# A hybrid diffusion backbone on one core: the layer-1 modulation product is summed per partition by VectorE and closed by TensorE, with changes to splits, a context write and the row ends

## The chip, the cores and the metric

The kernel runs on one core of a Trainium2 chip. The metric is the device time of one execution in microseconds, taken as the median of several runs. The engines are named as in the profile: PE is TensorE (PEld its weight loads), DVE is VectorE, ACT is ScalarE, POOL is GpSimd, and SP is the engine that issues nearly all DMA transfers. Each engine works through its own queue in order.

## What is computed

Two layers (`DEPTH` 2) of a backbone with 1024 features, 512 latent tokens and 256 context tokens. The modulation vector `c` (and `c_ctx` for the context) goes through one matrix per layer and yields six rows of 1024 features, which shift, scale and gate the two halves of a layer:

```python
mod   = silu(c)     @ w_mod[i] + b_mod[i]     # (1, 6 * 1024)
mod_c = silu(c_ctx) @ w_mod[i] + b_mod[i]
x = LN(alpha * x + gate1 * Mixer(modulate(x, shift1, scale1)))
x = LN(alpha * x + gate2 * (square(relu(h @ w1)) @ w2))   # h = modulate(x, shift2, scale2)
```

The mixer is one input projection, a conformer convolution, a bidirectional chunked state-space scan (SSD) and one output projection of 1536 to 1024 features. The MLP has 4096 hidden features. The output is the latent stream after two layers, in float32.

## The kernel before

**Matmuls and splits.** Every large matmul has float32 accuracy by three passes over operands that are split in a high and a low part. A weight unit of 512 KB is loaded to `raw`, cast by ScalarE to the high half of a buffer (L300), and the low half is the difference (L301), on VectorE, or for every third unit of an output projection on GpSimd (`sub_engine`, L272, unless `ostate["late"]` is set). The buffers are `spl`, of which there are three, and `splx`, which takes every fourth unit in output projections and MLPs. `weight()` keeps two units ahead.

**Output projection** (`outproj`, L849). Its left operand is split per feature block into `cr` (two buffers): the high half by ScalarE (L866), the low half alternately by GpSimd and VectorE (L868). TensorE's matmuls are L888. A finished half is multiplied by the gate, added to the residual and given to the row statistics on VectorE (L895 to L897). In layer 0 a first call does context and half of the latents (its branch ends with L910, which stops the modulation steps), a second call the rest; in the last layer there is no context.

**MLP** (`mlp`, L940). Eight chunks of 512 hidden features: the first matrix (L962), relu and square (L950 to L954), then the second matrix (L969), twelve tiles of twelve matmuls per chunk, each added to `acc` by VectorE (L1025). In the last chunks the residual is added (`residual`, L1202 to L1207) and `finish` (L1212) makes the row ends.

**Modulation.** The product for a layer is three parts of 2048 columns. A step (`mod_step`, L155) loads a row block of 128 x 2048 (1 MB, each partition one run of 8 KB) into an `spl` buffer under the name `mraw`, and makes four matmuls of 512 columns each with the two rows of `c` as the stationary operand, `tile_position` placing them in four column groups of the array (L160). After eight steps a part is complete in the PSUM bank `pm`; bias, transposes and the copies to `modT` and `grow` follow. Layer 1 needs 24 steps. They are queued in `fill` at the output projection of layer 0 and taken by `tick()` (L192), which is called after each block of work: at every tick in the first output projection (`FILLO` 1), at every fourth tick in the MLP (`FILLM` 4). The matmuls of a step follow three ticks behind the load (`MLAG`). What is left at chunk 6 is drained by `mod_rest`.

**Row ends.** In the last layer a finished row tile of 128 tokens is normalised: `FSPL` says how many of its 1024 columns VectorE does (0, 0, 512, 1024 for the four tiles); the rest is done by ScalarE (L1237) and GpSimd (L1238, L1239), then stored. GpSimd also makes each tile's `rsy`, the inverse standard deviation (L320). In layer 0, `finish` writes each pair of tiles as `xn` to memory with two GpSimd operations per tile (L1253, L1254), for latents and context.

The order on each engine comes from a scheduler that takes the operations by priority; `tc.cur_priority` shifts a stretch of code, and a higher number is later.

Of the kernel before, what the change touches and what calls it, by code (L numbers as in the profile page):

```python
# [7 lines left out]
F32 = mybir.dt.float32  # L8
# [7 lines left out]
DM = 1024  # L16
# [27 lines left out]
FILLM = 4  # L44
# [34 lines left out]
def block(ctx, tc, a):  # L79
# [40 lines left out]
    wdt = const.tile([128, DEPTH, 8, 32], F32, name="wdt")  # L120
    nhalf = const.tile([128, 8], F32, name="nhalf")
# [30 lines left out]
    def mod_step(l, part, kt, raw=None):  # L152
# [9 lines left out]
        if kt < 7:  # L162
            return
# [28 lines left out]
    def tick(mod_ok=True):  # L192
# [12 lines left out]
        if mod_wait and mod_wait[0][0] <= clock["t"]:  # L205
            mod_step(*mod_wait.popleft()[1])
        if mod_ok and fill and clock["t"] % clock["fill"] == 0:
            f = fill.popleft()
            lag = MLAG[state["x"] is not None]
            if lag:  # L210
                mod_wait.append((clock["t"] + lag, (*f, ahead(MPRI, mod_load, *f))))
            else:
                mod_step(*f)

    def mod_rest():
        while mod_wait:
            mod_step(*mod_wait.popleft()[1])
        while fill:
            mod_step(*fill.popleft())
# [629 lines left out]
    def outproj(l, cats, is_ctx, t0, pairs, xsrc, xdst, op, o2, group):  # L849
# [49 lines left out]
        if nt == 4:  # L899
            for hf in range(2):  # L900
# [9 lines left out]
                clock["fill"] = 10 ** 6  # L910
# [226 lines left out]
    for l in range(DEPTH):  # L1137
# [17 lines left out]
        with tc.tile_pool(name=f"x_{l}", bufs=1, reuse_waits="tile") as sx, \  # L1155
# [55 lines left out]

            def finish(t, ac, ps, hf, sl):  # L1212
# [9 lines left out]
                if hf == 0:  # L1222
                    return
                if last:
                    mv, y = row_rstd(sts[p][0], t % 2, 1)
                    c1 = FSPL[t]
                    for c in range(0, c1, FSTEP):
                        s2 = slice(c, min(c + FSTEP, c1))
                        V.scalar_tensor_tensor(ac[:, s2], ac[:, s2], mv[:, 0, 0:1], late["lg"][:, s2], op0=SUB, op1=MUL)
                        V.scalar_tensor_tensor(ac[:, s2], ac[:, s2], y, late["lb"][:, s2], op0=MUL, op1=ADD)  # L1230
                        Q.dma_start(a["out"][t * 128:(t + 1) * 128, s2], ac[:, s2])
                    if c1 == DM:
                        return
                    s2 = slice(c1, DM)
                    nb = small.tile([128, 2], F32, tag="bnb", name="bnb")[:, 0:1]
# [102 lines left out]
```

## Time and profile before

| what | us |
|---|---|
| median of 3 runs | 1962.62 |
| lowest, highest of them | 1962.42, 1970.56 |
| the profiled execution's own time | 1962.02 |
| its span in the trace | 1960.2 |

The stages on the trace are the first mixer to about 440 us, the output projection of layer 0 from there to 583, its MLP to about 1107, layer 1's mixer to 1499, its output projection to 1590 and its MLP to the end. A row of a timeline shows the start, the time that a group of like instructions took, engine, line, operation, result and operands; what stands in brackets is the idle time ahead of it and who ended it. Records of float32 matmuls on TensorE come in pairs for the modulation product (x2 is one matmul).

### The profile page before, as it was taken

The page shows a single profiled execution, that of the slowest core. Times are in us where ns is not written, and L with a number is a line of the kernel's source. Part 1 is how long each engine was busy: PE and PEld are TensorE (multiplying, and loading weights), DVE is VectorE, ACT ScalarE, POOL GpSimd, SP SyncE. Part 2 cuts the span into 40 slices and gives each one's busy share as a digit, 9 for nine tenths or more (in the row PEclk, how much of TensorE's full clock was granted, in tenths as well). Part 3 has the DMA queues.
Part 4 walks back from the last instruction along what each step waited for, and adds up shares of the span by engine and source line. Part 5 has one row for each costly group of instructions (what it writes and reads, how often), then busy time and mean ns, then how long its engine had stood idle before and what let it go on. Part 6 is the DMA issues. An engine that isn't in the chain of part 4 may idle for free.

```text
span 1960.2 us, 25875 instructions
## 1 busy us (share of the span) xinstructions
PE 1846.2 (94%) x9944; PEld 1512.3 (77%) x9944; DVE 1188.4 (61%) x1816; ACT 835.5 (43%) x1722; POOL 561.9 (29%) x467
## 2 busy tenths in 40 slices
PE   7999989988999999999999989989998989999997
PEld 4788878775778877877888867878885778888885
DVE  4898969767475233333336577988868563444465
ACT  3536556575474212212212245564665553222222
POOL 2234344523352000000003264545542530000035
PEclk9999999989999999999999999989998999999998
DMA  7434333434653433432323323222222733232331
GB/s 297 137 110 149 118 124 115 139 104 144 232 188 109 140 103 102 140 111 97 127 64 92 96 77 104 87 76 89 75 75 95 261 111 125 86 108 86 105 122 68
DMA packets 113516, 234.59 MB, mean 120 GB/s; under 512 B 7801, under 2 KB 52473, under 8 KB 107249
## 3 DMA queue, kind: packets, MB, share of 16 engines
q1 hardware_dynamic: 113392, 232.95, 36.0%
q8 instruction: 78, 1.28, 0.3%
q14 instruction: 46, 0.37, 0.1%
HBM read 221.15 MB, written 11.76 MB: 119 GB/s over the span
## 4 chain that ended last, share of the span: by engine, by line
PE 51%; POOL 6%; DVE 6%; issue 5%; ACT 4%; DMA 3%; SPq 0%; DVEq 0%; POOLq 0%; ACTq 0%
PE pa L962 19%; PE pa L969 18%; PE pa L888 5%; PE pa L337 4%; PE pa L644 2%; DMA b<-cs 1%; POOL spl L301 1%; PE pm L160 1%; ACT spl L300 1%; POOL xt L1204 1%; POOL xt L1205 1%; POOL rsy L320 1%; DMA raw<-w 1%; PE pb L727 1%; PE pb L732 1%
## 5 line engine op out<-in xcount | busy, mean ns | idle before, releaser
L969 PE MATMUL pa<-spl,hid 128*128 128x512 f32 x1440 | 352.2, 396 | 7.6 <-DVE hid L954 2.8
L300 ACT CAST spl<-raw 128x1024 fp32r<-128x1024 f32 x196 | 204.6, 1044 | 316.3 <-PE pa L969 198.3
L969 PEld LDWEIGHTS pa<-spl,hid 128*128 128x128 f32 x1440 | 268.5, 188 | 81.8 <-issue 10.9
L301 DVE TENSOR_TENSOR spl<-raw,spl 128x1024 fp32r<-128x1024 f32 x121 | 156.4, 1294 | 270.0 <-ACT spl L300 270.0
L337 PE MATMUL pa<-Hl,spl 128*128 128x512 f32 x1104 | 274.4, 399 | 1.8 <-DVE tmp L1217 1.7
L962 PE MATMUL pa<-Hl,spl 128*128 128x512 f32 (+1 forms) x1296 | 272.1, 367 | 0.8 <-DVE spl L301 0.8
L301 POOL TENSOR_TENSOR spl<-raw,spl 128x1024 fp32r<-128x1024 f32 x75 | 182.8, 2439 | 270.8 <-ACT spl L300 266.7
L962 PEld LDWEIGHTS pa<-Hl,spl 128*128 128x128 f32 x1296 | 222.9, 189 | 43.3 <-issue 4.2
L337 PEld LDWEIGHTS pa<-Hl,spl 128*128 128x128 f32 x1104 | 204.3, 190 | 52.1 <-issue 9.2
L953 POOL TENSOR_TENSOR rl<-rl 128x512 f32<-128x512 f32 (+2 forms) x18 | 27.1, 1504 | 659.4 <-ACT hid L952 654.1
L502 DVE SCALAR_TENSOR_TENSOR pc<-vp,pv,pc 128x768 f32<-128x768 f32 (+1 forms) x232 | 205.0, 884 | 3.3
L950 ACT ACTIVATE rl<-pa 128x256 f32<-128x256 f32 (+1 forms) x104 | 51.3, 498 | 281.4 <-PE pa L962 276.7
L1025 DVE TENSOR_TENSOR acc<-acc,pa 128x512 f32<-128x512 f32 x120 | 81.7, 685 | 119.1 <-PE pa L969 118.6
L888 PE MATMUL pa<-spl,cr 128*128 128x512 f32 x540 | 139.7, 407 | 10.9 <-POOL cr L868 5.1
L888 PEld LDWEIGHTS pa<-spl,cr 128*128 128x128 f32 x540 | 101.0, 192 | 38.5 <-POOL cr L868 7.4
L969 PE MATMUL pa<-splx,hid 128*128 128x512 f32 x480 | 125.6, 397 | 0.0
L337 PE MATMUL pa<-Hc,spl 128*128 128x256 f32 x816 | 117.8, 295 | 0.7 <-ACT t L479 0.7
L337 PEld LDWEIGHTS pa<-Hc,spl 128*128 128x128 f32 x816 | 105.8, 194 | 4.6 <-issue 1.7
L969 PEld LDWEIGHTS pa<-splx,hid 128*128 128x128 f32 x480 | 91.5, 191 | 19.9
L644 PE MATMUL pa<-spl,Hl 128*128 128x256 f32 x768 | 100.2, 288 | 0.0
L301 DVE TENSOR_TENSOR splx<-raw,splx 128x1024 fp32r<-128x1024 f32 x40 | 49.6, 1240 | 83.4 <-ACT splx L300 81.8
L644 PEld LDWEIGHTS pa<-spl,Hl 128*128 128x128 f32 x768 | 95.5, 194 | 0.3
(223 smaller groups left out, 2863.0 us busy)
## 6 DMA issues: line engine op xcount, KB each, us to landing
mraw<-w_mod SPq DMA_DIRECT2D x40, 1024.0 KB
raw<-w1c SPq DMA_DIRECT2D x64, 512.0 KB
raw<-w SPq DMA_DIRECT2D x64, 512.0 KB
raw<-w_col SPq DMA_DIRECT2D x48, 512.0 KB
raw<-w_out SPq DMA_DIRECT2D x48, 512.0 KB
b<-cs SPq DMA_DIRECT2D x40, 256.0 KB
E<-cs SPq DMA_DIRECT2D x40, 256.0 KB
w<-w_m SPq DMA_DIRECT2D x8, 1024.0 KB
```

What stands on the lines that cost most here:

```text
L160: T.matmul(ps[32 * j:32 * j + 32, :], lhsT=cst2[:, kt, :], rhs=raw[:, j * 512:(j + 1) * 512], start=(kt == 0), stop=(kt == 7), tile_positi ...
L300: S.copy(s[:, 0], raw)
L301: sub_engine(u, i).tensor_tensor(s[:, 1], raw, s[:, 0].bitcast(F32), op=SUB)
L337: T.matmul(ps[:, :n], lhsT=w[:, x, kt * 128:(kt + 1) * 128], rhs=H[:, kt, y, :], start=(kt == 0 and i == 0), stop=(kt == 7 and i == 2))
L502: V.scalar_tensor_tensor(o if j == KCONV - 1 else run["o"], vp[:, :, j:j + GRID], cw[:, j:j + 1], run["o"], op0=MUL, op1=ADD)
L644: T.matmul(ps[:, cc_ * 256:(cc_ + 1) * 256], lhsT=H[:, kt, y, o:o + 128], rhs=w[:, x, k4 * 256:(k4 + 1) * 256], start=(kt == 0 and i == 0) ...
L888: T.matmul(ps[j], lhsT=cr[:, y, j * 128:(j + 1) * 128], rhs=w[:, x, k * 512:(k + 1) * 512], start=(kp == OPAIRS[l][0] and k == 0 and i == ...
L950: S.activation(rl[:, a0 - c0:a1 - c0], p, AF.Relu)
L953: (V if m_ in SQV else G).tensor_tensor(rl[:, :m], rl[:, :m], rl[:, :m], op=MUL)
L962: T.matmul(ps, lhsT=w[:, x, kt * 128:(kt + 1) * 128], rhs=H[:, kt, y, t0:t1], start=(kt == 0 and i == 0), stop=(kt == 7 and i == 2))
L969: T.matmul(ps, lhsT=hid[k][:, y, t * 128:(t + 1) * 128], rhs=ws[k // 2][:, x, (k % 2) * 512:(k % 2 + 1) * 512], start=(k == 0 and i == 0), ...
L1025: V.tensor_tensor(acc[:, t, sl], acc[:, t, sl], ps, op=ADD)
```

## The change

In the first MLP the layer-1 modulation product no longer goes through TensorE in full. A load now brings a quarter of a part's columns for half of the rows: 512 rows by 512 columns as [128, 4 x 512], again 1 MB, in runs of 2 KB. VectorE multiplies each of the four row blocks by the partition's element of `c` (a per-partition scalar) and adds up in an accumulator `macc` of 128 x 512 (`mod_sums`); part 0, which is needed for both rows of `c`, has two accumulators. That is 128 operations. When both halves of a quarter are summed, one matmul per accumulator with a column of ones (`pick`) adds up the partitions into the same place of `pm` (`mod_close`, four ticks behind the second load). What follows a complete part is as before (`mod_end`). The quarters start with the MLP, at every third tick; none is taken in the output projection. The sums have a lower priority (`MODP` 50).

In the last layer's output projections all splits, of `cr` and of weights, are on VectorE. In layer 0 the context pair's `xn` isn't written, since layer 1 reads only the latents of it. In the last layer the third row tile's normalisation is held until the fourth's first half is finished, and GpSimd's operations there go by 512 columns.

```diff
-FILLM = 4
+FILLM = 3
+MODP = 50
+MODLAG = 4
...
+    def mod_sums(l, part, j, half, raw):
+        rows = 2 if part == 0 else 1
...
+        for k in range(4):
+            kt = 4 * half + k
+            for r, acc in enumerate(mod_ps[l, part, j]):
+                x = raw[:, k * 512:(k + 1) * 512]
+                if kt == 0:
+                    V.tensor_scalar(acc, x, cst2[:, kt, r:r + 1], None, op0=MUL)
+                else:
+                    V.scalar_tensor_tensor(acc, x, cst2[:, kt, r:r + 1], acc, op0=MUL, op1=ADD)
+
+    def mod_close(l, part, j):
+        accs = mod_ps.pop((l, part, j))
...
+        for r, acc in enumerate(accs):
+            T.matmul(ps[32 * j:32 * j + 32, :], lhsT=pick[:, r], rhs=acc, start=(r == 0), stop=(r == len(accs) - 1),
+                     tile_position=(0, 32 * j))
+        if j == 3:
+            mod_end(l, part, ps)
+
+    def mod_quarter(l, part, j, half):
+        raw = splp.tile([128, 2048], F32, tag="spl", name="mraw")
+        Q.dma_start(raw.rearrange("p (k c) -> p k c", k=4),
+                    a["w_mod"][l, half * 512:(half + 1) * 512, part * 2048 + j * 512:part * 2048 + (j + 1) * 512].rearrange(
+                        "(k p) c -> p k c", p=128))
...
+        mod_sums(l, part, j, half, raw)
...
+        if half:
+            mod_wait.append((clock["t"] + MODLAG, (l, part, j)))
...
-                clock["fill"] = 10 ** 6
                 if hf == 0:
                     load_res()
...
-            ostate["late"] = bool(LATE[2 if l == 0 else 3 if t0 == 0 else 4])
+            ostate["late"] = l == DEPTH - 1
...
-                fill.extend((1, p_, kt) for p_ in range(3) for kt in range(8))
-                clock["fill"] = FILLO or 10 ** 6
+                fill.extend((1, p_, j, h) for p_ in range(3) for j in range(4) for h in range(2))
+                clock["fill"] = 10 ** 6
...
+            def emit(t, ac, mv, y):
...
+                for c in range(c1, DM, FSTEP):
+                    s2 = slice(c, c + FSTEP)
+                    G.tensor_tensor(ac[:, s2], ac[:, s2], late["lg"][:, s2], op=MUL)
+                    G.tensor_tensor(ac[:, s2], ac[:, s2], late["lb"][:, s2], op=ADD)
...
+                    if held:
+                        emit(*held.pop())
                     return
                 if last:
...
+                    args = (t, ac, *row_rstd(sts[p][0], t % 2, 1))
+                    if t == n_tok - 2:
+                        held.append(args)
+                    else:
+                        emit(*args)
                     return
...
-                for j in range(2):
+                for j in range(2 if p > 0 or l + 1 < DEPTH - 1 else 0):
```

Three places show how the instructions stand now. First TensorE, in the first MLP, from the end of chunk 0's second matrix into chunk 1. Before (L160 is the modulation step, L962 and L969 the two matrices):

```order
L969 MATMUL pa<-splx,hid 128x512 x6
L969 MATMUL pa<-spl,hid 128x512 x6
L969 MATMUL pa<-splx,hid 128x512 x6
L962 MATMUL pa<-Hc,spl 128x256 x24
L962 MATMUL pa<-Hl,spl 128x512 x4
L160 MATMUL pm<-mraw,cst_90 32x512 x4
L962 MATMUL pa<-Hl,spl 128x512 x20
L962 MATMUL pa<-Hc,spl 128x256 x24
L962 MATMUL pa<-Hl,spl 128x512 x24
L160 MATMUL pm<-mraw,cst_90 32x512 x4
L962 MATMUL pa<-Hc,spl 128x256 x8
L173 MATMUL pb<-cst,ms 128x128 x4
```
After (L193 is the closing matmul, L1006 and L1013 the two matrices):

```order
L1013 MATMUL pa<-splx,hid 128x512 x4
L193 MATMUL pm<-macc,pick 32x512 x2
L1013 MATMUL pa<-splx,hid 128x512 x2
L1013 MATMUL pa<-spl,hid 128x512 x6
L1013 MATMUL pa<-splx,hid 128x512 x6
L1006 MATMUL pa<-Hc,spl 128x256 x24
L1006 MATMUL pa<-Hl,spl 128x512 x24
L1006 MATMUL pa<-Hc,spl 128x256 x24
L1006 MATMUL pa<-Hl,spl 128x512 x24
L1006 MATMUL pa<-Hc,spl 128x256 x24
L1006 MATMUL pa<-Hl,spl 128x512 x24
L1006 MATMUL pa<-Hc,splx 128x256 x24
```
Steps of four matmuls stood inside the first matrix; now a quarter's close of two matmuls, one for each row of `c`, stands near the end of the second matrix.

Second VectorE, in the first MLP, from chunk 0's hidden features to chunk 1's. Before (L301 is a weight split, L953 and L954 make the hidden features):

```order
L953 TENSOR_TENSOR rl<-rl 128x256
L954 TENSOR_TENSOR hid<-rl,hid 128x256
L301 TENSOR_TENSOR spl<-raw,spl 128x1024 x2
L301 TENSOR_TENSOR splx<-raw,splx 128x1024
L301 TENSOR_TENSOR spl<-raw,spl 128x1024
L954 TENSOR_TENSOR hid<-rl,hid 128x768
```
After (L183 and L185 are the sums, L346 a weight split, L998 the hidden features):

```order
L997 TENSOR_TENSOR rl<-rl 128x256
L998 TENSOR_TENSOR hid<-rl,hid 128x256
L183 TENSOR_SCALAR macc<-mraw,cst_90 128x512 x2
L185 SCALAR_TENSOR_TENSOR macc<-mraw,cst_90,macc 128x512 x14
L346 TENSOR_TENSOR spl<-raw,spl 128x1024 x2
L346 TENSOR_TENSOR splx<-raw,splx 128x1024
L183 TENSOR_SCALAR macc<-mraw,cst_90 128x512 x2
L185 SCALAR_TENSOR_TENSOR macc<-mraw,cst_90,macc 128x512 x6
L998 TENSOR_TENSOR hid<-rl,hid 128x768
```
Sixteen sums of the first quarter now stand ahead of chunk 1's weight splits, and those of the next behind them.

Third GpSimd, in the last layer's output projection, from the start of it to the row tiles' inverse deviations. Before (L301 weight splits, L868 `cr`, L320 `rsy`):

```order
L320 TENSOR_TENSOR rsy<-ssq,nhalf 128x2
L301 TENSOR_TENSOR spl<-raw,spl 128x1024
L868 TENSOR_TENSOR cr<-cat,cr 128x256 x2
L301 TENSOR_TENSOR splx<-raw,splx 128x1024
L868 TENSOR_TENSOR cr<-cat,cr 128x256
L301 TENSOR_TENSOR spl<-raw,spl 128x1024
L868 TENSOR_TENSOR cr<-cat,cr 128x256 x2
L301 TENSOR_TENSOR spl<-raw,spl 128x1024
L868 TENSOR_TENSOR cr<-cat,cr 128x256
L301 TENSOR_TENSOR spl<-raw,spl 128x1024
L868 TENSOR_TENSOR cr<-cat,cr 128x256
L320 TENSOR_TENSOR rsy<-bve,nhalf 128x2
```
After, from the same `rsy` to the next:

```order
L365 TENSOR_TENSOR rsy<-ssq,nhalf 128x2
L365 TENSOR_TENSOR rsy<-bve,nhalf 128x2
L1248 TENSOR_TENSOR xt<-xt,lg 128x512
L1249 TENSOR_TENSOR xt<-xt,lb 128x512
L1248 TENSOR_TENSOR xt<-xt,lg 128x512
L1249 TENSOR_TENSOR xt<-xt,lb 128x512
```
Splits and `cr` are gone from it, the residual's operations `xt` follow at once; they stand in VectorE's queue.

## Rows read from the trace of the kernel before

**Rows 1.** The page: engine, busy us, share of the span, instructions.

```profile
PE 1846.2 (94%) x9944; PEld 1512.3 (77%) x9944; DVE 1188.4 (61%) x1816; ACT 835.5 (43%) x1722; POOL 561.9 (29%) x467
```

**Rows 2.** Busy time by stage: window, its length, PE, PEld, DVE, ACT, POOL, clock, DMA.

```profile
440.00:583.00 143.00, 129.56 (x591) 95.18 (x589) 92.14 (x154) 81.86 (x173) 59.26 (x52) 0.99 0.56 190
...
690.00:750.00 60.00, 60.00 (x295) 45.64 (x295) 18.36 (x22) 11.23 (x15) 1.71 (x1) 1.00 0.34 113
...
1499.00:1545.00 46.00, 40.85 (x166) 31.50 (x167) 26.92 (x36) 22.15 (x35) 18.41 (x13) 0.94 0.59 203
1545.00:1590.00 45.00, 39.40 (x184) 31.26 (x183) 30.62 (x42) 25.39 (x42) 20.80 (x13) 0.96 0.47 157
```

**Rows 3.** The same view of line L160 alone: PE and PEld, records, clock, DMA.

```profile
440.00:583.00 143.00, 9.32 (x40) 1.22 (x40) 0.99 0.56 190
583.00:690.00 107.00, 3.20 (x24) 0.47 (x24) 1.00 0.35 119
690.00:1000.00 310.00, 21.21 (x128) 3.04 (x128) 1.00 0.33 111
```

**Rows 4.** Timeline of PE, first MLP: start us, us, instruction.

```profile
698.26 1.05 PE L160 MATMUL pm<-mraw,cst 128*32 128x512 f32 x2
699.24 1.21 PE L969 MATMUL pa<-spl,hid 128*128 128x512 f32 x4
...
701.36 12.64 PE L969 MATMUL pa<-spl,hid 128*128 128x512 f32 x54
...
716.45 1.07 PE L160 MATMUL pm<-mraw,cst 128*32 128x512 f32 x8
```

**Rows 5.** One source line over the whole run: min, median, max in ns.

```profile
L1207 DVE SCALAR_TENSOR_TENSOR acc<-xt,acc x20: 691/693/1757, 1058.6 to 1908.8; 128x512 f32<-128x512 f32 x20
```

**Rows 6.** Waits, 583 to 1170 us: who, for whom: total us, times, longest.

```profile
DVE spl L301 <- ACT spl L300: 152.7, 37, 14.5
...
PEld pm L160 <- DMA mraw<-w_mod: 3.3, 9, 0.4
```

**Rows 7.** Timelines of SP's queue and POOL: issues of loads and a first use.

```profile
711.28 0.33 SPq L149 DMA_DIRECT2D mraw<-w_mod  x1
...
1906.46 2.11 SPq L291 DMA_DIRECT2D raw<-w  x2
...
1910.22 2.39 POOL L294 TENSOR_TENSOR raw<-raw,gr 128x1024 f32<-128x1024 f32 x1 [9.75 <-DMA raw<-w]
```

**Rows 8.** Timeline of PE, first output projection.

```profile
484.45 1.15 PE L764 MATMUL pb<-cst,y 128*128 128x128 f32 x4 [4.02 <-ACT y L757]
485.53 1.94 PE L160 MATMUL pm<-mraw,cst 128*32 128x512 f32 x8
...
507.02 1.05 PE L160 MATMUL pm<-mraw,cst 128*32 128x512 f32 x2
```

**Rows 9.** Last layer's output projection: waits, then timelines of DVE and PE.

```profile
PE pa L888 <- POOL cr L868: 4.8, 3, 3.7
...
PE pa L888 <- DVE cr L868: 3.2, 3, 1.5
...
1508.90 2.23 DVE L868 TENSOR_TENSOR cr<-cat,cr 128x256 fp32r<-128x256 f32 x1 [0.29 <-ACT cr L866]
...
1516.03 1.22 DVE L301 TENSOR_TENSOR splx<-raw,splx 128x1024 fp32r<-128x1024 f32 x1
1518.51 0.42 DVE L868 TENSOR_TENSOR cr<-cat,cr 128x256 fp32r<-128x256 f32 x1 [1.27 <-ACT cr L866]
...
1576.58 5.68 PE L888 MATMUL pa<-spl,cr 128*128 128x512 f32 x17 [3.68 <-POOL cr L868]
```

**Rows 10.** Timeline of POOL at the start of layer 1.

```profile
1182.31 2.39 POOL L1253 TENSOR_TENSOR xn<-acc,lg 128x1024 f32<-128x1024 f32 x1 [1.37 <-ACT acc L829]
```

**Rows 11.** Timeline of POOL in the tail.

```profile
1950.09 0.54 POOL L320 TENSOR_TENSOR rsy<-bve,nhalf 128x1 f32<-128x1 f32 x1
1951.75 1.26 POOL L1238 TENSOR_TENSOR acc<-acc,lg 128x512 f32<-128x512 f32 x1 [1.12 <-ACT acc L1237]
```

More of the change, by code (lines that the diff above doesn't have):

```diff
@@ L120, in block @@
     wdt = const.tile([128, DEPTH, 8, 32], F32, name="wdt")
+    pick = const.tile([128, 2, 32], F32, name="pick")
+    G.memset(pick, 0.0)
+    for r in range(2):
+        G.memset(pick[:, r, r:r + 1], 1.0)
     nhalf = const.tile([128, 8], F32, name="nhalf")
@@ L161, in mod_step, with mod_end @@
                      start=(kt == 0), stop=(kt == 7), tile_position=(0, 32 * j))
-        if kt < 7:
-            return
+        if kt == 7:
+            mod_end(l, part, ps)
+    def mod_sums(l, part, j, half, raw):
+        rows = 2 if part == 0 else 1
+        if half == 0:
+            mod_ps[l, part, j] = [state["mp"].tile([128, 512], F32, tag="macc", name="macc", bufs=3)
+                                  for _ in range(rows)]
+        for k in range(4):
[8 more added lines that the diff above has]
+        accs = mod_ps.pop((l, part, j))
+        if j == 0:
+            mod_ps[l, part] = psM.tile([128, 512], F32, tag="M", name="pm")
+        ps = mod_ps[l, part]
+        for r, acc in enumerate(accs):
+            T.matmul(ps[32 * j:32 * j + 32, :], lhsT=pick[:, r], rhs=acc, start=(r == 0), stop=(r == len(accs) - 1),
+                     tile_position=(0, 32 * j))
+        if j == 3:
+            mod_end(l, part, ps)
+    def mod_quarter(l, part, j, half):
[3 more added lines that the diff above has]
+                        "(k p) c -> p k c", p=128))
+        p = tc.cur_priority
+        tc.cur_priority = p + MODP
+        mod_sums(l, part, j, half, raw)
+        tc.cur_priority = p
+        if half:
+            mod_wait.append((clock["t"] + MODLAG, (l, part, j)))
+    def mod_end(l, part, ps):
+        c0 = part * 2048
         ms = small.tile([128, 512], F32, tag="misc", name="ms")
@@ L1210, in residual @@
                     late["lb"] = load_row(o2, "lb", a["lnr"][l, 3:4])
+            held = []
+            def emit(t, ac, mv, y):
+                c1 = FSPL[t]
+                for c in range(0, c1, FSTEP):
+                    s2 = slice(c, min(c + FSTEP, c1))
+                    V.scalar_tensor_tensor(ac[:, s2], ac[:, s2], mv[:, 0, 0:1], late["lg"][:, s2], op0=SUB, op1=MUL)
+                    V.scalar_tensor_tensor(ac[:, s2], ac[:, s2], y, late["lb"][:, s2], op0=MUL, op1=ADD)
+                    Q.dma_start(a["out"][t * 128:(t + 1) * 128, s2], ac[:, s2])
+                if c1 == DM:
+                    return
+                nb = small.tile([128, 2], F32, tag="bnb", name="bnb")[:, 0:1]
+                V.scalar_tensor_tensor(nb, mv[:, 0, 0:1], -1.0, y, op0=MUL, op1=MUL)
+                S.activation(ac[:, c1:DM], ac[:, c1:DM], AF.Identity, bias=nb, scale=y)
+                for c in range(c1, DM, FSTEP):
+                    s2 = slice(c, c + FSTEP)
+                    G.tensor_tensor(ac[:, s2], ac[:, s2], late["lg"][:, s2], op=MUL)
+                    G.tensor_tensor(ac[:, s2], ac[:, s2], late["lb"][:, s2], op=ADD)
+                Q.dma_start(a["out"][t * 128:(t + 1) * 128, c1:DM], ac[:, c1:DM])
             def finish(t, ac, ps, hf, sl):
```

32 lines of the change are left out of this document (7 added, 25 removed).

## The prediction

> **What bounds the kernel now.** I read the page's engine lines first, then the busy time by stage, then the timelines of the stages that the diff touches. TensorE is busy 94% of the span, VectorE 61% [rows 1]. The table by stage says where TensorE can be helped and how: in the first MLP it is busy 60.00 of 60 us, so there only less TensorE work saves time, while VectorE works 18.36 us of 60 and has room [rows 2]. In the first output projection TensorE is busy 129.56 of 143 us, and in the last layer's output projection 80.25 of 91: there 13.4 and 10.8 us are waits, which other engines decide [rows 2]. The layer-1 modulation product is the TensorE group L160; its records by stage are 9.32, 3.20 and 21.21 us, 5, 3 and 16 steps of four matmuls (two records each) [rows 3].
>
> **The change part by part.**
>
> *The MLP on TensorE.* Removed are 19 steps (3 + 16), 24.41 us of records [rows 3]. Records overlap a little: a block of eight has 1.07 us, and 698.26 to 699.24 is 0.98 us from start to start [rows 4]. About a quarter of the steps are split in two by MLP matmuls, each piece paying its own 0.98 us: 24 pieces, 23.7 us. Added are 16 closing matmuls (eight for part 0, which has two rows of c, four for each other part). What does one cost? The row with one matmul (x2 records) has 1.05 us, the one with four (x8) 1.07 [rows 4]: a column group alone costs as much as four together. So 16 x 0.98 = 15.7 us, and the product falls from 96 matmuls to 16 but only from 23.7 to 15.7 us: **-8.0** (from -7.5 if the blocks are less split, to -8.7 by records). The Trainium skill, "TensorEngine Tiling (Array Packing)", Key Properties, states it as a rule that tiles of the array run in parallel, and adds that a change of the tiling mode drains the engine. The first half speaks against this change, whose closes use one tile of four, and gives the same -8.0; the second would make 14 switches in place of 24 worth something more, but no row shows a gap at a switch, so nothing is counted for it.
>
> *The MLP on VectorE.* Added are 128 operations 128x512: 16 multiplies by a scalar and 112 multiply-adds. The same multiply-add takes 0.693 us alone (1.757 at most, beside GpSimd) [rows 5]; with the multiplies priced alike, from above, that is 128 x 0.69 = 88 us, in a stage of some 460 us in which VectorE is idle two thirds of the time [rows 2]. GpSimd hardly works there, so 0.69 holds. As a sum this is hidden. As an order it isn't quite: VectorE's queue is in order, and accumulator adds, hidden-layer squares and weight splits now stand behind sums that wait for a load. Their cover: VectorE itself waits 152.7 us for ScalarE's casts in this stretch [rows 6], which are made as soon as a buffer is free, well ahead of use, and the accumulator adds have four PSUM buffers, 11 us at 2.8 us a tile (54 matmuls take 12.64 us [rows 4], a tile has 12).
>
> *When the closes come.* Each close stands on TensorE four ticks behind its second quarter's load. By the new order seven of the fourteen groups stand just behind the time at which they can be ready: a buffer of three is freed when five and a half to six of the block's twelve tiles are done, 15 to 16.5 us into it, the load takes about 5.2 us (711.28 to 716.45 for 1 MB in long rows) [rows 4, 7], then 4 or 8 sums take 2.8 to 5.5 us. That lands within about a microsecond of the close, so I add 0.4 us for each of the seven: **+3**. The new loads have 2 KB runs, which the trace shows only for loads of half the size: 3.76 us from issue to use [rows 7]. So a new load takes between 3.76 and 7.5 us (twice that); I take 5.2, nearest to the row of the same size. The bounds are 0 (no wait at all) and 7 x 2.3 + 3 = +19.
>
> *The first output projection.* Five steps leave it, 9.32 us of TensorE [rows 3]. Three blocks of about 1 us behind 487 us (507.02 is the first) [rows 8] stand in dense work and come back whole: 3.0 us. The one at 485.53, 1.94 us, stands just ahead of the next block and comes back if that block's weights are there [rows 8]; they are then no longer queued on SP behind a modulation load. The earlier ones lie among waits for VectorE's scan work, which is late anyway: I count a third of their 4.4 us. The 4.02 us wait at 484.45 [rows 8] gets eleven projection matmuls in front of it, worth up to as much, but the data for them must be there too; I count nothing. Sum **-6** (-3 to -11).
>
> *The last layer's output projection.* 12 splits of cr and about 8 weight splits move from GpSimd to VectorE. VectorE pays 12 x 0.42 + 8 x 1.22 = 15 us [rows 9], and there are 33 us of its time free (26.92 of 46 and 30.62 of 45 busy) [rows 2]. It gets back what sharing cost it: a cr split took 2.23 us beside a GpSimd weight split, 0.42 alone [rows 9]. TensorE waits 4.8 us there for cr splits on GpSimd and 3.2 us for those on VectorE, 8.0 us; the largest, 3.68, is for a GpSimd cr [rows 9]. cr has two buffers, one is used up in 2.8 us, and weight splits and a row block's evacuation now stand in the same queue, so new waits of a microsecond come in place of some. **-3** (-8 to +4). The Trainium skill, "GPSIMD Engine Reference", Specifications, says that GpSimd shares its SBUF interfaces with VectorE where the latter reads two SBUF tensors; the trace agrees (0.42 against 2.23 us), and by the rule alone the whole 8.0 us would go.
>
> *The context rows' xn in layer 0.* Four GpSimd operations of 2.39 us [rows 10] and two stores vanish at the start of layer 1, where nobody on TensorE waits for them; the weight splits between them come earlier: **-1** (-4 to +3, which also holds what a new order does to the mixer's start).
>
> *The row ends.* VectorE's and ScalarE's order in the tail is as before. GpSimd's two 1024-wide operations become four 512-wide ones, 1.26 us each against 2.39 [rows 10, 11], so a row's pair grows by 0.1 to 0.25 us, and the next row's rsy waits behind it in GpSimd's queue (1950.09) [rows 11]: **+0.4** (0 to +1).
>
> *Sum.* -8.0 + 3 - 6 - 3 - 1 + 0.4 = -14.6. The profiled execution took 1962.02 us (span 1960.2 plus 1.8 around it), so 1947.4; the median of the runs is 0.6 above it: **1948 us**, 0.75% faster. 0.5% (9.8 us) is about what a measurement of this kernel can tell from no change.
>
> **The rivals.**
>
> A. *The sums become the bound, slower.* If 2 KB runs land late, VectorE stands at a sum with accumulator adds and splits behind it, and seven closes wait. The price is 7 us for each us by which a close is late; it eats the whole 14.6 from 2.1 us on. With a load at 7.5 us (+2.3) and a split and an add ahead of the sums (1.23 + 0.69) it is 4.2 x 7 = 29 us: 1977 us. For it: buffers free late, and TensorE already waits 0.37 us at nine of the loads [rows 6]. Against: half-size loads with the same runs take 3.76 us.
>
> B. *The MLP gains nothing.* The 8 us of cheaper closes are eaten by waits of about 1.1 us at each of the seven, what is left is the output projections and ends, -6.6 without the rest of the waits: 1955 us. For it: a lone column group at full price, and closes placed without slack.
>
> C. *The last layer's splits backfire.* VectorE takes the row-block evacuations, transposes and all splits in one queue, and cr waits there: +4 in place of -3, 1955 us. For it: cr is needed every 2.8 us; against: a third of VectorE's time is free.
>
> D. *The row ends don't hold anything.* Holding the third row back changes no order on VectorE or ScalarE, so this part doesn't do what it says; the time is the forecast's within 0.5 us. It is in the sum.
>
> **How the numbers follow.** Forecast with its own scatter, 1940 to 1954: 0.56. B 0.20, C 0.10, both around 1955, a third of them just under the bound of 1952.8. A 0.14, of which five in six end above 1972.4, the rest between. Faster: 0.56 x 0.85 + 0.30 x 0.3 = 0.57. Slower: 0.12. Same: 0.31. The range leaves out nearly all of A and the low end, where the output projections give their most (-11 and -8): 1939 to 1964.
>
> **What the new profile would show.** In the MLP: closes of about 1 us, sums of 0.69 us on VectorE with VectorE busy some 33 us of 60, TensorE still full but for at most seven waits under a microsecond on a sum; waits of 2 us or more there mean A or B. In the first output projection: no modulation product, 137 us or so in place of 143. In the last one: no cr on GpSimd, VectorE's cr at 0.42, TensorE's waits down from 10.8 to 7 or 8; waits on VectorE's cr above 10 us mean C. In the tail: GpSimd at 1.26 us pieces and nothing else new. Wrong would be a multiply-add well above 0.69 us, a load above 6 us, or a close that costs clearly less than 1 us.

## The result and the profile after

The changed kernel takes 1952.74 us (median of 5 runs, 1952.1 to 1954.77) against 1962.62 us for the kernel before beside it (1959.63 to 1970.56). The ratio is 0.994 with a 95% interval of 0.9917 to 0.9963, so it is between 0.4 and 0.8% faster. The forecast was 1948 us with a range of 1939 to 1964. Measured once more in another comparison, the changed kernel took 1948.04 us against 1963.4 us (0.9927, 0.9903 to 0.995); a kernel's median moves by some microseconds from one comparison to the next, so the ratios to the kernel before of the same comparison are the safer numbers.

The profiled execution has a span of 1951.0 us, 9.2 less than before. The page's engine line answers to [rows 1]; VectorE has gone from 61 to 66%, TensorE's records from 1846.2 to 1835.5 us:

```profile
PE 1835.5 (94%) x9784; PEld 1518.8 (78%) x9784; DVE 1279.5 (66%) x1963; ACT 836.5 (43%) x1722; POOL 524.1 (27%) x451
```

The busy time by stage answers to [rows 2] (window, length, PE, PEld, DVE, ACT, POOL, clock, DMA). The first output projection is no denser and runs at a granted clock of 0.94 in place of 0.99. In the MLP VectorE works 39.98 us of 60 and TensorE 58.32. In the last layer's output projection TensorE is busy 75.3 of 80 us, which was 80.25 of 91:

```profile
440.00:583.00 143.00, 125.31 (x553) 98.42 (x552) 89.99 (x151) 81.99 (x174) 57.68 (x52) 0.94 0.46 157
690.00:750.00 60.00, 58.32 (x264) 43.98 (x263) 39.98 (x64) 9.53 (x12) 2.40 (x2) 1.00 0.36 124
1493.00:1539.00 46.00, 43.08 (x174) 33.67 (x175) 31.06 (x49) 22.87 (x36) 2.25 (x3) 0.90 0.60 211
1539.00:1573.00 34.00, 32.23 (x145) 25.24 (x144) 28.86 (x41) 21.96 (x39) 8.65 (x5) 1.00 0.57 187
```

**Where the 9.2 us went**, by the starts of the same matmuls of TensorE in the two traces. Up to the first output projection -2.0; nothing in the change reaches there, and in the traces of the other kernels that point lies anywhere from 435.3 to 445.1 us. First output projection and the MLP's first matrix blocks: 182.96 us before, 184.98 now, +2.0. The eleven blocks of the first MLP in which modulation stood: -5.1. From there through the mixer of layer 1: -0.3 (the first MLP's own matmuls run to about 1165 us in the trace of the kernel before, not to 1107). The last layer's output projection, from the broadcast of `rsy` that follows its first three matmuls to the MLP's first matmul: 85.38 us before, 77.82 now, -7.6. The last MLP and the tail: +3.8. The eleven blocks run from the first matmul of chunk 0's second matrix to that of chunk 6's first matrix, 394.45 us before and 389.32 us now. The rows are the starts of the first output projection, of the eleven blocks, of what follows them, and of the last output projection and MLP (timeline of PE, kernel before, then after):

```profile
440.09 3.10 PE L888 MATMUL pa<-spl,cr 128*128 128x512 f32 x12
...
623.05 1.30 PE L969 MATMUL pa<-spl,hid 128*128 128x512 f32 x5
...
1017.50 1.70 PE L962 MATMUL pa<-Hc,spl 128*128 128x256 f32 x13
...
1500.84 2.08 PE L552 MATMUL pa<-cst,rsy 128*128 128x128 f32 x8 [0.16 <-POOL rsy L320]
...
1586.22 6.16 PE L962 MATMUL pa<-Hl,spl 128*128 128x256 f32 x50
```

```profile
438.13 3.12 PE L933 MATMUL pa<-spl,cr 128*128 128x512 f32 x12
...
623.11 1.07 PE L1013 MATMUL pa<-spl,hid 128*128 128x512 f32 x4
...
1012.43 1.82 PE L1006 MATMUL pa<-Hc,spl 128*128 128x256 f32 x14
...
1495.45 2.08 PE L597 MATMUL pa<-cst,rsy 128*128 128x128 f32 x8 [0.16 <-POOL rsy L365]
...
1573.27 6.16 PE L1006 MATMUL pa<-Hl,spl 128*128 128x256 f32 x50
```

The closes of the changed kernel answer to [rows 3] and [rows 4]. First line L193 alone from 623 to 1050 us (PE and PEld busy, clock, DMA): 16 matmuls take 16.33 us where 19 steps took 24.41. Then three closes in TensorE's timeline: the first of part 0, two matmuls in four records for one quarter (one for each row of `c`), and the two that waited longest on the sums, 1.44 and 1.59 us:

```profile
623.00:1050.00 427.00, 16.33 (x32) 2.36 (x32) 1.00 0.36 120
```

```profile
653.18 1.90 PE L193 MATMUL pm<-macc,pick 128*32 128x512 f32 x4 [0.16 <-DVE macc L185]
...
720.31 1.05 PE L193 MATMUL pm<-macc,pick 128*32 128x512 f32 x2 [1.44 <-DVE macc L185]
...
951.54 1.04 PE L193 MATMUL pm<-macc,pick 128*32 128x512 f32 x2 [1.59 <-DVE macc L185]
```

VectorE's sums answer to [rows 5] and the loads to [rows 7]: the first load is issued at 638.41 and its first multiply starts at 643.64, 5.2 us later, and eight multiply-adds take 5.39 us together, 0.67 each from start to start. By the measure of [rows 5], the duration of one, the multiply-add has a median of 0.747 us. Not every load is so quick: the sums at 715.53, for which VectorE sat idle, read the load that was issued at 709.06, 6.5 us earlier (timelines of SP's queue and of DVE). The wait row is TensorE's on the sums from 623 to 1112 us, 3.4 us in four places:

```profile
638.41 1.75 SPq L200 DMA_DIRECT2D mraw<-w_mod  x2
...
709.06 20.72 SPq L200 DMA_DIRECT2D mraw<-w_mod  x3
```

```profile
643.64 0.88 DVE L183 TENSOR_SCALAR macc<-mraw,cst 128x512 f32<-128x512 f32 x2 [16.52 <-DMA mraw<-w_mod]
...
715.53 5.39 DVE L185 SCALAR_TENSOR_TENSOR macc<-mraw,cst,macc 128x512 f32<-128x512 f32 x8 [1.65 <-DMA mraw<-w_mod]
```

```profile
PE pm L193 <- DVE macc L185: 3.4, 4, 1.6
```

The place in the first output projection that [rows 8] show, in TensorE's timeline after, and ScalarE's operations ahead of the weight cast it waits for:

```profile
485.15 1.15 PE L809 MATMUL pb<-cst,y 128*128 128x128 f32 x4 [4.42 <-ACT y L802]
488.16 7.50 PE L933 MATMUL pa<-splx,cr 128*128 128x512 f32 x24 [1.86 <-ACT splx L345]
```

```profile
484.59 0.91 ACT L802 ACTIVATE y<-y,rsy 128x256 f32<-128x256 f32 x2 [1.86 <-POOL rsy L365]
486.34 0.84 ACT L709 ACTIVATE cat<-pb,pv 128x256 f32<-128x256 f32 x2 [0.84 <-PE pb L809]
487.07 1.04 ACT L345 CAST splx<-raw 128x1024 fp32r<-128x1024 f32 x1
```

The 4 us wait for `y` is still there (4.42). Where the modulation step stood, TensorE now waits 1.86 us for the cast of `splx`. That cast stands in ScalarE's queue behind the last part of the scan: `y` waits for GpSimd's `rsy`, `cat` for the product of `y`. So the block starts when the scan lets it, with or without a step: from the start of the product of `y` to that of the block it is 3.01 us in both traces (484.45 to 487.46 in the kernel before, 485.15 to 488.16 now), and in all the kernels below, except 2.96 us in the one with fillers at this very place. And then it runs slowly: 24 matmuls take 7.50 us, 5.89 before.

### The profile page after: what moved, and what is told of

The parts are those of the page before. It is cut to its first block, busy times and chain, and to the rows that moved or that the text cites. A ratio compares the mean times of both kernels' runs of the same rounds, so it can differ in the third digit from the quotient of the medians.

```text
span 1951.0 us, 25655 instructions
## 1 busy us (share of the span) xinstructions
PE 1835.5 (94%) x9784; PEld 1518.8 (78%) x9784; DVE 1279.5 (66%) x1963; ACT 836.5 (43%) x1722; POOL 524.1 (27%) x451
## 5 line engine op out<-in xcount | busy, mean ns | idle before, releaser
L345 ACT CAST spl<-raw 128x1024 fp32r<-128x1024 f32 x196 | 204.7, 1044 | 376.8 <-PE pa L1013 159.3
L1013 PE MATMUL pa<-spl,hid 128*128 128x512 f32 x1440 | 352.8, 397 | 9.1 <-DVE spl L346 2.9
L1013 PEld LDWEIGHTS pa<-spl,hid 128*128 128x128 f32 x1440 | 269.9, 189 | 79.7 <-DVE hid L998 5.0
L346 DVE TENSOR_TENSOR spl<-raw,spl 128x1024 fp32r<-128x1024 f32 x126 | 160.8, 1278 | 179.1 <-ACT spl L345 178.1
L1006 PE MATMUL pa<-Hl,spl 128*128 128x512 f32 (+1 forms) x1296 | 271.4, 366 | 0.9 <-DVE spl L346 0.9
L1006 PEld LDWEIGHTS pa<-Hl,spl 128*128 128x128 f32 x1296 | 223.2, 188 | 40.8 <-issue 1.7
L346 POOL TENSOR_TENSOR spl<-raw,spl 128x1024 fp32r<-128x1024 f32 x70 | 169.2, 2419 | 262.5 <-ACT spl L345 252.7
L1013 PE MATMUL pa<-splx,hid 128*128 128x512 f32 x480 | 126.5, 398 | 0.0
L1013 PEld LDWEIGHTS pa<-splx,hid 128*128 128x128 f32 x480 | 91.7, 192 | 21.7 <-issue 1.7
L346 DVE TENSOR_TENSOR splx<-raw,splx 128x1024 fp32r<-128x1024 f32 x42 | 53.5, 1274 | 61.7 <-ACT splx L345 60.8
```

The lines of the kernel that those rows point to most:

```text
L345: S.copy(s[:, 0], raw)
L346: sub_engine(u, i).tensor_tensor(s[:, 1], raw, s[:, 0].bitcast(F32), op=SUB)
L1006: T.matmul(ps, lhsT=w[:, x, kt * 128:(kt + 1) * 128], rhs=H[:, kt, y, t0:t1], start=(kt == 0 and i == 0), stop=(kt == 7 and i == 2))
L1013: T.matmul(ps, lhsT=hid[k][:, y, t * 128:(t + 1) * 128], rhs=ws[k // 2][:, x, (k % 2) * 512:(k % 2 + 1) * 512], start=(k == 0 and i == 0), ...
```

## The experiments

Times of a kernel are compared with those of the kernel before in the same comparison; stages are read from one trace each. "The eleven blocks" are those of the rows above.

**1. No modulation in the first output projection, nothing else.**

```diff
 # kernel before
-FILLO = 1
+FILLO = 0
```

> The kernel before, but no modulation step in the first output projection: all 24 steps of four matmuls are in the first MLP. Theory of the gaps: the steps stood in gaps of TensorE and kept its granted clock up, so without them the output projection takes 143.4 us as before, with a granted clock under 0.9 between 440 and 480 us, and the MLP pays for five more steps, +5 to +6: about 1968 us. The prediction's own view (9.32 us of TensorE leave the stage, 6 come back): the stage takes 137 us and the whole time is within 1 us of before. Third view, the loss came from quarter loads or VectorE's sums ahead of the MLP: the stage takes 137 us here, since there are none.

Measured: 1970.36 us against 1963.42 (ratio 1.0045, 1.0031 to 1.0059). The output projection takes 143.45 us; the changed kernel has 143.49, and three kernels that kept the steps there have 143.40, 145.69 and 145.71. The first splx block takes 7.57 us here too. Between 440 and 480 us the granted clock is 0.87, as the theory of the gaps had it; three kernels that kept the steps have 1.00, 0.91 and 0.91. The eleven blocks take 398.89 us, 4.4 more than before, with 21 steps in them in place of 19; three more steps stand behind them. The place of [rows 8] in this kernel:

```profile
484.54 1.15 PE L764 MATMUL pb<-cst,y 128*128 128x128 f32 x4 [4.43 <-ACT y L757]
487.55 7.57 PE L888 MATMUL pa<-splx,cr 128*128 128x512 f32 x24 [1.86 <-ACT splx L300]
```

So five steps in that output projection cost nothing, and in the MLP the five cost 6.9 us, 1.4 each (1.2 to 2.3 by the interval). With no quarter load and no sum in this kernel, the third view is out: the missing gain isn't due to them. The prediction's own -6 is out as well.

**2. TensorE work without a reader put back there.**

```diff
 # changed kernel
+    def filler(cr):
+        ps = psM.tile([128, 512], F32, tag="M", name="pm")
+        for j in range(4):
+            T.matmul(ps[32 * j:32 * j + 32, :], lhsT=cst2[:, 0, :], rhs=cr[:, 0, :].bitcast(F32), start=True, stop=True,
+                     tile_position=(0, 32 * j))
...
-                        matmuls(ps, ahead(CRP, split, kp + k, cl), w, kp, k)
+                        cr = ahead(CRP, split, kp + k, cl)
+                        matmuls(ps, cr, w, kp, k)
+                        if hf == 0 and 0 < 2 * OPAIRS[l].index(kp) + k < 6:
+                            filler(cr)
```

> The changed kernel, with five groups of four matmuls without a reader (two columns of c against the high half of cr, 512 columns, into the free modulation bank) in the first half of the first output projection, about where the modulation steps stood. No load, no VectorE work. Theory of the gaps and the clock: the granted clock is back at 1.00 between 440 and 500 us, the part up to the first splx matmul takes 47 us in place of 50, the stage 141 in place of 143.5, and the whole is 2 to 3 us faster than the changed kernel, about 1950 us, although TensorE has 5 us more to do. Rival, VectorE's scan work alone bounds that part: the stage stays at 143.5 us, whatever the clock. Rival, TensorE is bound there: 5 us slower, 1958 us.

Measured: 1945.75 us against 1963.42 (0.9916, 0.9896 to 0.9935). The fillers take 7.38 us of records (line L234, window, PE, PEld, clock, DMA), and the part up to the first splx block takes 48.35 us, the output projection 142.78 and all up to the MLP's second matrix 182.36, 2.6 us under the changed kernel's trace:

```profile
440.00:500.00 60.00, 7.38 (x32) 1.02 (x32) 0.91 0.32 109
...
485.55 1.15 PE L815 MATMUL pb<-cst,y 128*128 128x128 f32 x4 [4.37 <-ACT y L808]
488.56 8.49 PE L939 MATMUL pa<-splx,cr 128*128 128x512 f32 x24 [1.86 <-ACT splx L351]
```

Traces without fillers or steps have 182.34 to 185.05 us for that stretch, so no gain is shown. But more than seven microseconds of TensorE work went in for nothing, so TensorE is not the bound there: that part of the theory stands. The clock part is half right. Between 440 and 480 us the granted clock is 1.00 as expected, but that shortened nothing; and the splx block, still behind two idle stretches of 4.37 and 1.86 us, is as slow as before (8.49 us). The 7 us against the changed kernel's first measurement are not explained by the stage; experiment 9 and the repetition (10) take that up.

**3. The last layer's splits alone.**

```diff
 # kernel before
-            ostate["late"] = bool(LATE[2 if l == 0 else 3 if t0 == 0 else 4])
+            ostate["late"] = l == DEPTH - 1
```

> The kernel before with one part of the change alone: the last layer's output projection makes all its splits on VectorE. If the gain read from the trace (7.5 us there) is this part's own, TensorE's waits on cr fall from 8.0 us to about 1.2 and the whole time by 4 to 8 us: 1955 to 1958 us. If the last MLP's loss of 3 us (a later weight split at its first second-layer block, then a lower clock) belongs to this part, it shows here too and the sum is -4; if it belongs to something else, the sum is -7.5. The prediction took -3: 1959.6 us.

Measured: 1956.45 us against 1963.42 (0.9969, 0.9952 to 0.9985), 3 to 9 us. The last output projection takes 80.17 us, which was 85.38. TensorE's waits on cr are 1.2 us in place of the 8.0 of [rows 9] (waits between 1499 and 1586 us: who, for whom, total, times, longest):

```profile
PE pa L888 <- DVE cr L868: 1.2, 2, 0.6
```

The first block pair of the last MLP takes 50.2 us, as before: the loss there isn't this part's.

**4, 5 and 6. Closing four column groups together.** In all three the accumulators lie in the residual's row buffers, which are idle in this stage; 4 and 5 differ in the lag, 5 and 6 in the grouping alone, so 6 keeps the changed kernel's `mod_close`.

```diff
 # changed kernel
-            mod_ps[l, part, j] = [state["mp"].tile([128, 512], F32, tag="macc", name="macc", bufs=3)
-                                  for _ in range(rows)]
+            if rows == 2 or j % 2 == 0:
+                state["mt"] = state["mp"].tile([128, DM], F32, tag="r", name="macc", bufs=RB)
+            mt = state["mt"]
+            mod_ps[l, part, j] = [mt[:, 0:512], mt[:, 512:DM]] if rows == 2 else [mt[:, (j % 2) * 512:(j % 2 + 1) * 512]]
...
     def mod_close(l, part, j):
+        if j < 3:
+            return
+        accs = [mod_ps.pop((l, part, q)) for q in range(4)]
...
+        for r in range(rows):
+            for q in range(4):
+                T.matmul(ps[32 * q:32 * q + 32, :], lhsT=pick[:, r], rhs=accs[q][r], start=(r == 0), stop=(r == rows - 1),
+                         tile_position=(0, 32 * q))
...
-            state["mp"] = fp
+            state["mp"] = o2
...
-MODLAG = 4
+MODLAG = 10   # 5 (grouped) and 6 (one by one)
```

> The changed kernel, but a part's four column groups are closed together, when its last quarter is summed: the same 16 closing matmuls in five places in place of fourteen; the accumulators lie in the residual's idle row buffers. If a lone column group costs what four cost (1.05 us), L160's successor falls from 16.3 us to about 5 us and the MLP gains 11 us, plus up to 3.4 us of waits on sums: 1939 to 1943 us. If the closing matmuls cost by their number instead, nothing changes: 1952 us. If VectorE's sums bound the MLP by now, the gain comes back as waits on splits and adds: 1948 us or more.

Measured: 1945.22 us against 1963.42 (0.9919, 0.9898 to 0.994). The closes take 7.00 us of records, but the last of them waited 4.42 us on its sums, and its first matmul then took 1.92 us; that block took 42.4 us where an undisturbed one takes 33.4. The eleven blocks take 384.3 us, and the whole is above the 1939 to 1943 us expected. So the theory holds for the closes, but that one block lost 9 us: the wait is 4.42 of them, the rest are the close itself with its transposes and matmuls that ran at a granted clock of 0.50 from 942 to 948 us (line L197, then TensorE's timeline):

```profile
623.00:1050.00 427.00, 7.00 (x32) 1.02 (x32) 0.99 0.37 124
...
942.09 1.92 PE L197 MATMUL pm<-macc,pick 128*32 128x512 f32 x2 [4.42 <-DVE macc L187]
```

> The grouped closes of the run before (four column groups of a part closed together, accumulators in the idle row buffers), but ten ticks behind the last load in place of four, since there one close waited 4.4 us on a sum and its block took 42.4 us in place of 33.4. If a lone column group costs as much as four, and the sums are off TensorE's path once nothing waits for them, the eleven blocks of the first MLP from 623 us on take about 372 us in place of 389 in the changed kernel (33.0 and 33.4 us undisturbed, 365 in all, plus 5 us of closes and their transposes), and the whole about 1936 us. If VectorE's queue holds the blocks up, the wait turns up at splits and adds and the eleven blocks stay above 380 us.

> The changed kernel with its closes one column group at a time, but ten ticks behind the load and with the accumulators in the idle row buffers: the twin of the grouped run, the two differ only in the grouping. The waits of TensorE on sums, 3.4 us in the changed kernel, go; 16 closing matmuls at 1.05 us remain: the eleven blocks take 384 to 386 us, the whole about 1949 us, and the grouped twin is 11 to 12 us faster. If closes cost by their number, the twins are equal.

Measured: grouped 1941.32 us, one by one 1949.14 us, both against 1964.04 (0.9893, 0.987 to 0.9916; 0.9921, 0.9893 to 0.9948). The eleven blocks take 377.20 and 387.07 us, and the closes 6.34 and 15.98 us. Here are the closes' line and the two ends of the blocks, of the grouped kernel and then of its twin:

```profile
623.00:1050.00 427.00, 6.34 (x32) 0.89 (x32) 1.00 0.39 128
...
627.74 1.54 PE L1016 MATMUL pa<-spl,hid 128*128 128x512 f32 x6
...
1004.94 1.22 PE L1009 MATMUL pa<-Hc,spl 128*128 128x256 f32 x9
```

```profile
623.00:1050.00 427.00, 15.98 (x32) 2.53 (x32) 1.00 0.38 124
...
624.78 1.54 PE L1015 MATMUL pa<-spl,hid 128*128 128x512 f32 x6
...
1011.85 1.34 PE L1008 MATMUL pa<-Hc,spl 128*128 128x256 f32 x10
```

The same sixteen matmuls differ by 9.6 us of TensorE and 9.9 us of the blocks. The whole times are 7.8 us apart, less than the 11 to 12 expected, and their intervals overlap at the edge; the blocks are the safer reading. Neither kernel waits on a sum any more. Both are 1 to 5 us above what was expected of the blocks: TensorE waits 2.6 and 2.1 us there for hidden features. At the longest of these waits in the grouped kernel, 1.50 us, VectorE makes them behind a weight split that waited for ScalarE's cast; the rest was not followed up.

**7. The changed kernel with the old splits.**

```diff
 # changed kernel
-            ostate["late"] = l == DEPTH - 1
+            ostate["late"] = False
```

> The changed kernel with the last layer's splits divided between GpSimd and VectorE as before: undoes one part. If the parts add up, the last output projection is back at 85 us from 77.8 and the whole is 6 to 7 us slower than the changed kernel, 1959 us, and 4 to 5 us faster than the kernel before, which is then what the modulation part with the rest is worth. If the gain of the splits was only one execution's, no difference: 1953 us.

Measured: 1958.32 us against 1964.04 (0.9979, 0.9962 to 0.9996). The last output projection is back at 85.56 us, and the waits on cr are those of before, almost to the digit:

```profile
PE pa L933 <- POOL cr L913: 4.8, 3, 3.7
PE pa L933 <- DVE cr L913: 3.5, 3, 1.5
```

With experiment 3 the parts add up within their intervals: the splits alone are worth 0.31%, everything else 0.21%, the whole change 0.6 to 0.7%.

**8. The two small parts alone.** The edit is the change's own `emit`, `held` and the shorter `xn` loop in the kernel before.

```diff
 # kernel before
-                for j in range(2):
+                for j in range(2 if p > 0 or l + 1 < DEPTH - 1 else 0):
...
+                    if t == n_tok - 2:
+                        held.append(args)
+                    else:
+                        emit(*args)
```

> The kernel before with the two small parts alone: no context xn in layer 0, and the row ends' new order with GpSimd's operations by 512 columns. The prediction took -1 and +0.4. From the end of the first MLP's last first-matrix block to the last output projection 386 to 388 us (387.7 and 390.3 in the two runs with the writes, 384.9 to 387.4 in those without), the tail within 1 us of 44. The whole between 1960 and 1964 us; a difference of more than 4 us would mean that one of the two carries a share of the gain that was given to the others.

Measured: 1963.34 us against 1964.04 (0.9996, 0.998 to 1.0011). No difference can be told, and none was priced above 1 us. The trace does tell one: from the end of the last MLP's last matmul to the end of the span it is 10.9 us here, which was 10.3 in the kernel before.

**9 and 10. Filling only the idle stretches ahead of the first splx block, and the changed kernel again.**

```diff
 # 9: the filler of experiment 2, twice each, at these places only
+                        if hf == 0 and 6 <= 2 * OPAIRS[l].index(kp) + k <= 7:
+                            filler(cr)
+                            filler(cr)
```

> The changed kernel with four groups of four matmuls without a reader put only into the two idle stretches of TensorE (4.4 and 1.86 us) ahead of the first splx block of the first output projection; the rest of TensorE's order is the changed kernel's. In the seven traces taken so far without modulation steps there, that block ran at a granted clock of 0.75 to 0.84 where the clock could be read and took 7.2 to 8.5 us, in the kernels with them 5.9 to 6.1. If the idle time ahead of it is what lowers the clock, the block takes about 6 us here, the stretch from its start to the MLP's second matrix falls from 134.9 us to 133 or less, and the fillers cost nothing. If the block is slow for another reason (its weights, the port), it stays above 7 us.

> The changed kernel itself once more, on the chip and beside the runs of this call, since the run with fillers came out 7 us under it in another call although their instructions differ in the output projection alone. If that was the chip, this gives 1946 to 1948 us and the first block pair of the last MLP takes 50.4 us; if it was the fillers, it stays at 1952 to 1954 us.

Measured: 1948.75 and 1948.04 us, both against 1963.4 (0.9927, 0.9903 to 0.9952 and to 0.995). The block itself answers clearly. TensorE's timeline and the stretch from 490 to 500 us (window, length, PE, PEld, DVE, ACT, POOL, clock, DMA), with the fillers and then without:

```profile
482.69 2.22 PE L234 MATMUL pm<-cr,cst 128*32 128x512 f32 x16
...
488.01 2.20 PE L234 MATMUL pm<-cr,cst 128*32 128x512 f32 x14
490.15 5.77 PE L939 MATMUL pa<-splx,cr 128*128 128x512 f32 x24
...
490.00:500.00 10.00, 10.00 (x47) 8.12 (x44) 2.82 (x4) 3.09 (x7) 3.80 (x3) 1.00 0.94 345
```

```profile
486.62 1.15 PE L809 MATMUL pb<-cst,y 128*128 128x128 f32 x4 [4.42 <-ACT y L802]
489.63 7.56 PE L933 MATMUL pa<-splx,cr 128*128 128x512 f32 x24 [1.86 <-ACT splx L345]
...
490.00:500.00 10.00, 10.00 (x37) 8.06 (x37) 1.69 (x3) 2.38 (x5) 2.53 (x3) 0.82 0.05 14
```

With the stretches filled the block takes 5.77 us at a granted clock of 1.00, the upper of the two levels (2.4 GHz), and without them 7.56 us at a mean of 0.82 in that stretch and of 0.74 over the block alone (489.63 to 497.19 us), so partly at the lower one (1.2 GHz). That shows it: what slows the block is the idle time ahead of it. It isn't the traffic of the loads, of which the fast block has more beside it (345 against 14 GB/s). From there to the MLP's second matrix it is 133.37 against 134.33 us, where 133 or less was expected. In the whole time the microsecond can't be seen. With the repetition, experiment 2's lead is not shown: its 0.9916 and the changed kernel's 0.9927 have intervals that overlap. The first block pair of the last MLP takes 51.3 us in the repetition, not the 50.4 expected.

**11. Grouped, late closes with the fillers of experiment 2.** The edits are those above.

> The grouped closes, ten ticks late, with the five filler groups of the earlier run in the first output projection: the best of both. If the fillers' 7 us were theirs, 1934 to 1936 us; if they were the chip's or one execution's, 1941 us like the grouped run alone.

Measured: 1934.15 us against 1963.4 (0.9854, 0.9835 to 0.9872). It is 13.9 us under the changed kernel of the same comparison and beats both kernels clearly. Its eleven blocks take 376.8 us, as those of experiment 5, so some 12 us of the 14 are the grouping's; whether the fillers add 2 us or more is not settled, since grouped with and without them were not run in one comparison. The time is the one expected if the fillers count, but the changed kernel too was 4.7 us lower in this comparison than in the first.

## Why the prediction came out as it did

The time lay in the range and the direction was right; the sum was -14.6 and the result -9.9 in the first measurement, -15.4 in the second. Behind that stand two terms that were well off in opposite directions, the first output projection and the last layer's splits, and a loss in the last MLP that was not in the sum. That the total came so near is in part luck.

- **The MLP, -8.0 on TensorE and +3 of waits: right.** The eleven blocks lost 5.1 us against the forecast 5.0. Closes cost 16.33 us (forecast 15.7), a lone column group 1.05 us, and the waits on sums were 3.4 us (forecast 3). A slip in the working does no harm: 24 pieces of 0.98 us are 23.5 us and not 23.7, which makes the term -7.8. The Trainium skill, "TensorEngine Tiling (Array Packing)", Key Properties, says that the tiles of the array run in parallel; the twins agree with it, sixteen matmuls in 6.34 us grouped and in 15.98 us one by one.
- **The sums on VectorE: right in the sum, not in every load.** 0.67 us each in a row, priced at 0.69 (0.747 by the duration of one); over the eleven blocks VectorE is busy 214.3 of 389.4 us, the 33 of 60 that were forecast. The quick loads in 2 KB runs reached VectorE after 5.2 us, the value that was taken, but some came later than the 6 us that were named as a sign of being wrong, and the two longest waits of a close, 1.44 and 1.59 us, stand behind two of these (issued at 709.06 and 941.40, read 6.5 and 7.0 us later). So rival A's mechanism is there, at a small price: it and B fell because the closes waited 3.4 us in all, not 1.1 at each of seven places. B's own price was off: with nothing from the MLP the other terms leave -9.6 (1953 us), and its -6.6 adds the 3 us of waits once more.
- **The first output projection, -6: wrong.** From its start to the MLP's second matrix three traces with steps there have 182.96 to 185.29 us (kernel before, 3 and 8), seven without steps or fillers 182.34 to 185.05 (changed kernel, its repetition, 1, 4, 5, 6 and 7). The step that failed is twofold. Of the steps ahead of 487 us I counted a third of 4.4 us and one of 1.94 us as coming back; nothing came back, since ScalarE's queue, and behind it the scan, lets the splx block start no earlier (the ACT rows above, and the 3.01 us that are the same with and without a step). Of the three blocks behind it I counted all of 3.0 us; they are gone, but the block that follows the now longer idle time runs 1.6 us slower (7.50 against 5.89), because the clock had fallen, which experiment 9 shows. The rest is partly waited away at the rows `r` ahead of the MLP in this trace (3.30 us in place of 2.66), but not in the repetition (2.72).
- **The last layer's splits, -3: right in kind, too small.** The stage went from 85.38 to 77.82 us, and to 80.17 us with the splits alone (experiment 3). TensorE's waits on cr fell from 8.0 to 1.2 us; the new waits of a microsecond, for which I took 5 us off, hardly came, since VectorE's cr kept at 0.42 us (median of 24 below). The Trainium skill, "GPSIMD Engine Reference", Specifications, lists the SBUF interfaces as shared with VectorE where that reads two SBUF tensors; of the whole 8.0 us that this rule alone would have given, 6.8 came. Rival C fell. What it leaves is this (one source line after, ns; then the wait):

```profile
L913 DVE TENSOR_TENSOR cr<-cat,cr x24: 397/422/1511, 1470.8 to 1569.1; 128x256 fp32r<-128x256 f32 x24
```

```profile
PE pa L933 <- DVE cr L913: 1.2, 2, 0.7
```

- **xn, -1: nothing that can be told,** as experiment 8 has it. **The row ends, +0.4: right, by the traces.** From the end of the last MLP's last matmul to the end of the span the three traces with the old row ends have 10.3 us, the ten with the new ones 10.9. GpSimd's pair of 1024 columns takes longer in four pieces and `rsy` waits behind it as forecast (TensorE's last matmuls before and after, then POOL's timeline after, answering to [rows 11]). Rival D, that holding the row back does nothing by itself, fits that and was in the sum; the holding was not run by itself:

```profile
1948.36 1.54 PE L969 MATMUL pa<-splx,hid 128*128 128x512 f32 x6
```

```profile
1938.50 1.54 PE L1013 MATMUL pa<-splx,hid 128*128 128x512 f32 x6
```

```profile
1937.73 2.97 POOL L1273 TENSOR_TENSOR acc<-acc,lb 128x512 f32<-128x512 f32 x2
1940.66 0.55 POOL L365 TENSOR_TENSOR rsy<-bve,nhalf 128x1 f32<-128x1 f32 x1
```

- **The last MLP, forecast 0, +3.8 in the trace with the tail's 0.6: open.** In the changed kernel and those built on it its first block pair takes between 50.4 and 53.7 us, in the kernel before and the three built on it 50.2 to 50.4, and kernels with the same instructions there lie at both ends (experiment 2 at 50.4, the changed kernel at 53.7). Where it is long, GpSimd's square for the last hidden features stands behind residual operations whose load was issued some 1.5 us later, and TensorE then waits 2.9 us for a split behind those features in place of 1.4; the 52 matmuls behind that wait take 13.79 us in place of 12.18, at a mean granted clock of 0.88 in place of 1.00. What delays the load was not tried.

## What to carry to other kernels

A step of TensorE that stands in a stage where TensorE waits for others is free there; taking it away saves nothing, and may cost what the lower clock takes from the block behind the idle time. Ask of each removed instruction whether what comes next on its engine is ready at once. A reduction that is closed with narrow matmuls should be closed with all column groups together: one alone costs what four cost, here 10 us for sixteen matmuls.

## What was not expected of the hardware

A block of 24 matmuls behind idle stretches of 4.4 and 1.9 us took 7.2 to 8.5 us in all the traces that had those stretches, at a mean granted clock of 0.65 to 0.79 over the block itself, and 5.77 us at 1.00 when matmuls without a reader filled them. The stretch up to the first output projection, with the same work in every kernel, ended anywhere from 435.3 to 445.1 us: differences of that size between two single traces mean nothing, and a stage is better compared by its own length.
